# Stores of the scan's matrices and of the inverses issued by GpSimd instead of SyncE, in a hybrid DeltaNet, retention and attention encoder layer

## The chip, the cores and the metric

The kernel runs on one core of one Trainium2 chip. The core has TensorE (PE; its weight loads are listed as PEld), VectorE (DVE), ScalarE (ACT), GpSimd (POOL) and SyncE (SP). SP computes nothing; in this kernel it issues nearly all transfers. In the profile, transfers issued by SP are on queue q1 (hardware_dynamic) and those issued by GpSimd on q0 (software_dynamic); both are carried out by the core's 16 DMA engines. Each engine takes its instructions strictly in the order in which the program lists them for that engine, and waits at the head of its queue until the semaphores it needs are up.

The metric is device time in microseconds for one execution. Several runs are taken, and their median counts.

## What is computed

The reference applies one encoder layer to two sequences (1024 and 256 tokens of width 1024), with the same weights. After an RMS norm, one matrix multiplication projects to the inputs of three groups of heads; their outputs are gated, joined, multiplied by `w_out` and added to the input; a gated embedding term and a last RMS norm follow.

```
xn   = rms_norm(h, norm_g);  proj = xn @ w_in
A (6 heads): q, k, v = silu(conv5(a_qkv)); q, k normalized to length 1
             o = deltanet(q, k, v, beta, g) + the same on the reversed sequence
B (6 heads): retention, forward and reversed, then a head norm
C (4 heads): attention in a window of 128 to each side, with sink and ALiBi
h = h + concat(A, B, C, each times silu(gate)) @ w_out
h = h + (p @ w_ple) * sigmoid(h @ w_pg);  y = rms_norm(h, final_g)
```

The part around the change is group A. The gated delta rule works on chunks of 64 tokens:

```
gamma[c,s] = exp(decay[c] - decay[s]) for s <= c
T  = I + strict_lower((k*beta) k^T * gamma)       # 64 x 64 for each chunk and head
u, w = T^-1 (v*beta),  T^-1 (k*beta*exp(decay))
per chunk, in order:  v_new = u - w S
                      o = (q*exp(decay)) S + (q k^T * gamma) v_new
                      S = S * chunk_decay + (k*exp(decay_last - decay))^T v_new
```

So each chunk needs three matrices beside the inverse of T: the decayed queries, the masked products of q and k, and the decayed keys. The kernel calls them l2. They and the inverses go through DRAM: a preparation writes them, and the scan over the chunks reads them back.

## The kernel before

All products with the big weights are done in float32 as three products of a high and a low part. The kernel runs through these stages, with their approximate place in the profile:

- Load and normalize the input, transpose it to `xh` and `xl` (up to about 40 us).
- The products for the queries, keys and values of group A, with convolution, SiLU and normalization (L510 to L566). The order is `[3, 4, 5, 0, 1, 2, 6, 7, 8]` (L509): keys, queries, and last the values, which are transposed and stored to `VTD`. All nine come ahead of the preparation; the last ends about 218.
- The preparation, `prep_stream` (L569 to L627), about 218 to 347, interleaved by `spread` with ten other products of the input (`PP`, L37). It takes the ten blocks of 128 tokens from the last to the first, and each for two directions d. For each of the 20 pairs: GpSimd loads rows of decays into `DJ[d]` (L591; one tile for each direction), PE spreads them over 128 partitions (L595, the product sb), ScalarE makes the exponentials `ge` (L598, L601), VectorE multiplies the Gram products (L580, in the PSUM bank `sa`) with them into `at` (L609) and into `l2` (L611 to L613), and GpSimd copies the last decay (`elc`, L614). Then SP issues nine stores: four of `at` to `AGD` (L616, for the inversion), one to `ADD_` (L618, for the join), and four of `l2` to `L2D` (L620 for the upper 64 partitions, L623 three times for the lower). `at` and `l2` have two buffers each. In the profile `L2D` is l2d, `AGD` agd, `ADD_` ad, `YDD` yd and the tile `l2` is l.
- After five blocks, `invert(g)` (L399 to L426) for a group g of five blocks and both directions: the 32 x 32 diagonal blocks are read back from `AGD` (L402), VectorE inverts 120 of them for each direction (L411 to L421; the first instruction is one multiplication over 120x2048), and two stores write them to `YDD` (L426). A store takes 120 partitions with 32 rows of 32 elements each, out of rows of 33 elements. `invert(1)` runs between the pairs of the second five blocks and ends at 363; `invert(0)` follows and ends at 447.
- The scan, `scan_stream` (L751), from about 350 to 770: four `join`s (L652) for group 1, each making a part of the full 64 x 64 inverses from `YDD` (yn, L662, transposed to xn at L666) and `ADD_` (an, L659), then 20 steps for both directions (L695 to L749), in which SP loads l2, the inverse and the values, and GpSimd scales values (L702) and states (L726). `weave` and `fill` put window attention, the remaining products and retention beside it. Attention lets GpSimd cast queries (`qh`, L827).
- `w_out`, gate and last norm (about 790 to the end).

What sets the order: the generators hand over pieces in the order of their planned lengths (`T_PREP` = 10.0 for a block of the preparation, `T_JOIN` = 5.0, `T_STEP` = 10.0 and so on), and the framework's planner, which simulates the program (L47: `TCARGS = dict(schedule_with_timeline_sim=True)`), then lays out one fixed sequence for each engine. A piece marked `tc.high_priority()` (the loads at L402) is put ahead.

Through the helper `mm` nearly all products have line 86 in the profile, and through `tt` nearly all two-input operations have line 89; the tile names tell them apart.

Of the kernel before, what the change touches and what calls it, by code (L numbers as in the profile page):

```python
# [53 lines left out]
def encoder_kernel(ctx: ExitStack, tc: tile.TileContext, I, O, dbg=None, upto=99):  # L54
    nc = tc.nc
    uid = [0]

    def nm(s):
        uid[0] += 1
        return f"{s}_{uid[0]}"  # L60

    def bc(ap, shape):
        return ap.to_broadcast(list(shape))
# [5 lines left out]
    def ps(tag):  # L69
        return psp.tile([128, 512], F32, tag=tag, name=nm(tag))  # L70
# [14 lines left out]
    def mm(out, lhsT, rhs, start=True, stop=True):  # L85
        nc.tensor.matmul(out, lhsT, rhs, start=start, stop=stop)  # L86

    def tt(eng, out, a, b, op):
        eng.tensor_tensor(out=out, in0=a, in1=b, op=op)  # L89
# [30 lines left out]
    ot = big.tile([128, 8, PADW], F32, tag="OT", name="ot")  # L120
# [35 lines left out]
    def acc():  # L156
        wide.append(wide.pop(0))
        return ps(wide[-1])
# [216 lines left out]
    L2D = [[tc.dram_tile([2, 128, 3, 3, 64], F32, name=f"l2d{d}_{b}") for b in range(NB)] for d in range(2)]  # L375
# [3 lines left out]
    YDD = [[tc.dram_tile([120, 32, 32], F32, name=f"yd{d}_{g}") for g in range(2)] for d in range(2)]  # L379
# [5 lines left out]
    T, B = slice(0, 64), slice(64, 128)  # L385
# [11 lines left out]
    IREG = (0, 1)  # L397

    def invert(g):  # L399
        for d in range(2):  # L400
            with tc.high_priority():
                nc.sync.dma_start(out=ot[0:120, IREG[d], 0:1056].rearrange("p (a b) -> p a b", a=32),  # L402
                                  in_=AGD[d][g].rearrange("q c p r x -> (q c p) r x"))

        def two(o0, o1, *dims):

            a = ot[0:120, IREG[0], o0:o0 + 1]
            return bass.AP(a.tensor, a.offset, [list(a.ap[0]), [(IREG[1] - IREG[0]) * PADW + o1 - o0, 2], *([list(e) for e in dims])])

        y, yd = two(0, 0, (33, 32), (1, 32)), two(32, 32, (0, 32), (33, 32))  # L410
        tt(V, y, y, yd, MUL)  # L411
        yield 4.2
        for s in range(1, 31):
            na, nb = s, 31 - s
            t3 = two(1056, 1056, (nb, na), (1, nb))

            c = two(s, 33 * (32 - s) + 31 - s, (33, na), (0, nb))
            r = two(33 * s + s + 1, 33 * (31 - s), (0, na), (1, nb))
            o = two(s + 1, 33 * (32 - s), (33, na), (1, nb))
            tt(V, t3, c, r, MUL)  # L420
            tt(V, o, o, t3, ADD)  # L421
            if s % 3 == 0:
                yield 2.8
        V.memset(two(0, 0, (34, 32)), 1.0)
        for d in range(2):
            nc.sync.dma_start(out=YDD[d][g], in_=ot[0:120, IREG[d], 0:1056].rearrange("p (a b) -> p a b", a=32)[:, :, 0:32])  # L426

    def weave(*run):

# [66 lines left out]
    with tc.tile_pool(name="pa", reuse_waits="tile", bufs=2) as pa:  # L496
# [13 lines left out]
        for i, ti in enumerate(order):  # L510
# [18 lines left out]
            if ti < 6:  # L529
                p, isq = ti % 3, ti < 3  # L530
# [17 lines left out]
                if not isq:  # L548
                    nc.sync.dma_start(out=KND[:, :, p, :].rearrange("c p t -> p c t"),
                                      in_=kq[:, p, 0, :].rearrange("p (c t) -> p c t", c=NC))  # L550
            else:
                p = ti - 6
                for b0 in range(0, NB, 4):
# [7 lines left out]
                    for r in range(2):  # L561
# [4 lines left out]
                                      in_=vt[:, 0:nb].rearrange("p b r e -> p (b r) e"))  # L566
        if dbg:
            dbg("kq", kq)
        def prep_stream():  # L569
            for b in reversed(range(NB)):  # L570
                tb = slice(b * 128, (b + 1) * 128)
                g3 = []
                for r in range(2):
                    tk = slice(b * 128 + 64 * r, b * 128 + 64 * r + 64)
                    gram = ps("sa")
                    g3.append(gram[:, 0:384].rearrange("p (q w) -> p q w", q=3))
                    for p in range(3):
                        for h in range(2):
                            rw, o = slice(64 * h, 64 * h + 64), slice(64 - 64 * h, 128 - 64 * h)
                            mm(g3[r][o, p, :].rearrange("p (w t) -> p w t", w=2), kq[rw, p, 0, tk], kq[rw, p, :, tk])  # L580
                kt = ps("tr")
                kt3 = kt[:, 0:384].rearrange("p (q w) -> p q w", q=3)
                for p in range(3):
                    nc.tensor.transpose(kt3[:, p, :], kq[:, p, 0, tb], ident)
                kc = pa.tile([128, 2, 3, 64], F32, tag="kc", name=nm("kc"), bufs=1)
                for r in range(2):
                    for h, rw in ((1, T), (0, B)):
                        S.copy(kc[rw, r], kt3[64 * r:64 * r + 64, :, 64 * h:64 * h + 64])
                for d in range(2):
                    for l in range(2):  # L590
                        nc.gpsimd.dma_start(out=DJ[d][2 * l:2 * l + 2], in_=DRD[d][6 * b:6 * b + 6, l].rearrange("n (s t) -> s n t", s=2))  # L591
                    ge = pa.tile([128, 2, 2, 3, 64], F32, tag="ge", name=nm("ge"))
                    for i in range(2):
                        pd = ps("sb")
                        mm(pd[:, 0:384], SD[i], DJ[d].rearrange("r n t -> r (n t)"))  # L595
                        if i == 0:
                            for n in range(6):
                                S.activation(out=ge[:, 0, n // 3, n % 3], in_=pd[:, 64 * n:64 * n + 64], func=AF.Exp,  # L598
                                             bias=negd[:, d, 2 * b + n // 3, n % 3:n % 3 + 1])
                        else:  # L600
                            S.activation(out=ge[:, 1].rearrange("p c q t -> p (c q t)"), in_=pd[:, 0:384], func=AF.Exp)  # L601
                    at = pa.tile([128, 2, 3, 2, 33], F32, tag="at", name=nm("at"), bufs=AB)
                    l2 = pa.tile([128, 2, 3, 3, 64], F32, tag="l2", name=nm("l2"))
                    last = 63 if d == 0 else 0
                    gl = ge[:, 0, :, :, last:last + 1]
                    el = ge[:, 1, :, :, last:last + 1]
                    S.copy(at[:, :, :, :, 32], bc(nbeta[:, d, 2 * b:2 * b + 2, :].unsqueeze(3), [128, 2, 3, 2]))
                    for r in range(2):
                        tt(V, at[:, r, :, :, 0:32], g3[r][:, :, 0:64].rearrange("p q (w t) -> p q w t", w=2),  # L609
                           ge[:, 0, r].rearrange("p q (w t) -> p q w t", w=2), MUL)  # L610
                        tt(V, l2[:, r, 1], g3[r][:, :, 64:128], ge[:, 0, r], MUL)  # L611
                    tt(V, l2[:, :, 2], kc, bc(gl, [128, 2, 3, 64]), MUL)
                    tt(V, l2[:, :, 0], kq[:, :, 1, tb].rearrange("p q (c t) -> p c q t", c=2), ge[:, 1], MUL)  # L613
                    G.tensor_copy(elc[:, d, 2 * b:2 * b + 2, :], el.rearrange("p c q t -> p c (q t)"))  # L614
                    for q in range(4):
                        nc.sync.dma_start(out=AGD[d][b // 5][q, 2 * b % 10:2 * b % 10 + 2].rearrange("c p r x -> r (c p) x"),  # L616
                                          in_=at[32 * q:32 * q + 32, :, :, q % 2, :].rearrange("r c p x -> r (c p) x"))
                    nc.sync.dma_start(out=ADD_[d][b // 5][2 * b % 10:2 * b % 10 + 2].rearrange("c p q w t -> p c q w t"), in_=at)  # L618

                    nc.sync.dma_start(out=L2D[d][b][:, T].rearrange("r p a q t -> p r (a q t)"),  # L620
                                      in_=l2[T].rearrange("p r a q t -> p r (a q t)"))
                    for a, a2 in ((0, 1), (1, 0), (2, 2)):
                        nc.sync.dma_start(out=L2D[d][b][:, B, a2].rearrange("r p q t -> p r (q t)"),  # L623
                                          in_=l2[B, :, a].rearrange("p r q t -> p r (q t)"))
                    yield T_PREP / 2
                if b % 5 == 0:
                    yield from invert(b // 5)  # L627


        for _ in spread((10 * T_PREP + 2 * 32.2, prep_stream()), length(PP)):  # L630
            pass
# [504 lines left out]
    with tc.tile_pool(name="fw", reuse_waits="tile", bufs=2) as fw:  # L1136
# [21 lines left out]
        for gi in range(2):  # L1158
            c0 = WSEQ[gi][1]
            w = wf.pop()  # L1160
            for i, b in enumerate(range(NB) if gi else FO):
                tk = slice(b * 128, (b + 1) * 128)
                p = acc()
# [22 lines left out]
        for gi in range(2):  # L1186
# [10 lines left out]
            for b in range(NB):  # L1197
                tk = slice(b * 128, (b + 1) * 128)
                end = gi == 1 and b == NB - 1
                for j, (o, n) in enumerate(((0, 256), (256, 256)) if end else ((0, 512),)):  # L1200
                    cs = slice(o, o + n)
                    p = acc()
# [50 lines left out]
```

## Time and profile before

| | us |
|---|---|
| Median of three runs (1092.92 to 1097.69) | 1095.28 |
| The profiled execution | 1089.95 |
| Its span, first to last instruction | 1088.2 |
| Issuing of l2d stores by SP, first to last | 221.4 to 346.8 |
| Issuing of yd stores by SP, two pairs | 362.7 and 447.1 |
| Mean granted TensorE clock | 0.963 |

How to read it: busy shares are means over the whole span, while the change touches only the preparation and the start of the scan. For these, the table of stages and the instructions in order of time are the views to look at. In a line of the latter stand the start, the length, the engine (SPq is SP's queue), the source line, the operation, what it writes and reads, the count and, in brackets, how long the engine stood idle before it and what ended that. The granted clock is the share of full speed that TensorE was allowed. Instructions that issue transfers are not counted as busy time of an engine, and a transfer's time to landing is given where it is known.

### The profile page before, as it was taken

What the parts mean: (1) busy time and instruction counts of PE and PEld (TensorE: products, weight loads), DVE (VectorE), ACT (ScalarE), POOL (GpSimd) and SP (SyncE); (2) the same over time, 40 slices, a digit from 0 to 9 for tenths busy, and PEclk for the clock granted to TensorE, in tenths of its full rate; (3) what the DMA queues carried; (4) which work ended last, traced back from release to release, by engine and by line L of the source; (5) the groups of instructions that cost most, each with busy time, mean ns of one, the idle gap of its engine ahead of it and who ended that gap; (6) DMA issues with size and microseconds to landing.
All of it is one profiled execution on the core that took longest, in us unless ns stands there. A gap on an engine that the chain in (4) does not pass through costs nothing.

```text
span 1088.2 us, 20996 instructions
## 1 busy us (share of the span) xinstructions
PE 1016.4 (93%) x7859; PEld 810.3 (74%) x7859; DVE 626.0 (58%) x1303; ACT 513.6 (47%) x1194; POOL 241.5 (22%) x406
## 2 busy tenths in 40 slices
PE   4999999999798789999998899989799999999996
PEld 4768878888687677877786777767567888888885
DVE  6766676454688588755566764665873333412333
ACT  8476776577467444443444322323341121534544
POOL 2001000022122111221233325554441000112311
PEclk9999999999899889999999799999879999999998
DMA  8112112377778734553555434555461430300211
GB/s 257 38 44 69 45 39 59 74 176 162 184 169 215 162 83 111 118 140 89 121 140 135 117 85 139 147 141 153 126 212 49 171 100 1 97 1 11 98 78 77
DMA packets 199071, 120.57 MB, mean 111 GB/s; under 512 B 105906, under 2 KB 180442, under 8 KB 198970
## 3 DMA queue, kind: packets, MB, share of 16 engines
q1 hardware_dynamic: 194074, 118.97, 41.1%
q8 instruction: 62, 1.02, 0.4%
q0 software_dynamic: 4896, 0.27, 0.4%
q14 instruction: 39, 0.32, 0.1%
HBM read 76.26 MB, written 42.91 MB: 110 GB/s over the span
## 4 chain that ended last, share of the span: by engine, by line
PE 45%; DVE 4%; DMA 2%; POOL 1%; issue 1%; ACT 1%; SPq 0%; DVEq 0%; POOLq 0%; ACTq 0%
PE mm L86 19%; PE sa L86 14%; PE sb L86 6%; PE tr L86 3%; DVE ot L968 2%; PE tr L850 1%; PE tr L1175 1%; POOL oo L89 1%; DMA oo<-od 1%; PE tr L949 1%; DMA od<-os 0%; DMA ot<-in_x_prompt 0%; DMA oo<-ond 0%; PE sa L1034 0%; DVE sab L1020 0%
## 5 line engine op out<-in xcount | busy, mean ns | idle before, releaser
L86 PE MATMUL mm<-xh,whi 128*128 128x512 f32 x720 | 265.6, 369 | 3.5 <-ACT ot L520 1.1
L86 PE MATMUL mm<-xl,whi 128*128 128x512 f32 x720 | 263.2, 366 | 0.0
L86 PE MATMUL mm<-xh,wlo 128*128 128x512 f32 x720 | 261.2, 363 | 0.0
L86 PEld LDWEIGHTS mm<-xh,whi 128*128 128x128 f32 x720 | 137.3, 191 | 29.1 <-ACT ot L520 2.2
L86 PEld LDWEIGHTS mm<-xl,whi 128*128 128x128 f32 x720 | 137.4, 191 | 20.7 <-issue 0.7
L86 PEld LDWEIGHTS mm<-xh,wlo 128*128 128x128 f32 x720 | 137.2, 191 | 20.7 <-issue 0.5
L89 DVE TENSOR_TENSOR ot<-ot 128x1284 f32<-128x1284 f32 (+16 forms) x131 | 85.7, 654 | 23.1 <-ACT ot L102 15.1
L89 DVE TENSOR_TENSOR wlo<-raw,whi 128x1024 fp32r<-128x1024 f32 (+1 forms) x56 | 57.4, 1028 | 32.1 <-ACT whi L149 19.8
L86 PE MATMUL mm<-whi,xh 128*128 128x512 f32 (+1 forms) x168 | 67.9, 406 | 0.6 <-ACT xh L1040 0.4
L86 PE MATMUL mm<-whi,xl 128*128 128x512 f32 (+1 forms) x168 | 67.4, 401 | 0.3 <-DVE xl L89 0.3
L86 PE MATMUL mm<-wlo,xh 128*128 128x512 f32 (+1 forms) x168 | 67.3, 401 | 0.0
L86 PE MATMUL sa<-wlo,xh 128*128 128x512 f32 (+1 forms) x160 | 62.8, 392 | 0.0
L86 PE MATMUL sa<-whi,xl 128*128 128x512 f32 (+1 forms) x160 | 62.6, 391 | 0.0
L86 PE MATMUL sa<-whi,xh 128*128 128x512 f32 (+1 forms) x160 | 62.4, 390 | 0.0
L525 DVE SCALAR_TENSOR_TENSOR ot<-ot,cols 128x1284 f32<-128x1284 f32 x36 | 55.9, 1554 | 0.6
L89 DVE TENSOR_TENSOR sgm<-sb,sgm 128x512 f32<-128x512 f32 (+1 forms) x21 | 14.0, 666 | 72.6 <-ACT sgm L102 60.2
L86 PE MATMUL sa<-sv,l 128*64 128x64 f32 (+1 forms) x912 | 47.0, 238 | 7.4 <-DVE sv L732 5.4
L86 PEld LDWEIGHTS sa<-sv,l 128*64 128x64 f32 (+1 forms) x912 | 36.7, 144 | 18.7 <-DVE sv L732 7.2
L89 POOL TENSOR_TENSOR sv<-sv,elc 64x192 f32<-64x192 f32 x72 | 38.9, 540 | 49.4 <-PE sa L86 26.7
L89 POOL TENSOR_TENSOR ot<-ot,sgm 128x512 f32<-128x512 f32 x19 | 25.5, 1342 | 100.0 <-DVE sgm L89 98.6
L89 POOL TENSOR_TENSOR vt<-vt,sab 128x192 f32<-128x192 f32 x40 | 23.2, 587 | 84.7 <-DMA vt<-vtd 67.7
L86 PEld LDWEIGHTS mm<-whi,xh 128*128 128x128 f32 x168 | 32.4, 194 | 8.2 <-ACT xh L1040 0.6
(302 smaller groups left out, 1975.5 us busy)
## 6 DMA issues: line engine op xcount, KB each, us to landing
raw<-in_w_in SPq DMA_DIRECT2D x28, 512.0 KB, 3.8
l<-l2d SPq DMA_DIRECT2D x40, 288.0 KB, 3.0
l2d<-l SPq DMA_DIRECT2D x20, 288.0 KB
l2d<-l SPq DMA_DIRECT2D x60, 96.0 KB, 3.0
xt<-in_x_prompt SPq DMA_DIRECT2D x8, 512.0 KB, 6.8
ot<-in_x_prompt SPq DMA_DIRECT2D x8, 512.0 KB
raw<-in_w_pg SPq DMA_DIRECT2D x16, 256.0 KB, 3.1
yp<-ot SPq DMA_DIRECT2D x8, 512.0 KB, 2.6
```

Of the source, the lines that this page charges most:

```text
L86: nc.tensor.matmul(out, lhsT, rhs, start=start, stop=stop)
L89: eng.tensor_tensor(out=out, in0=a, in1=b, op=op)
L525: V.scalar_tensor_tensor(out=Y[:, 0:1284], in0=R[:, j:j + 1284], scalar=cw(ti, j), in1=Y[:, 0:1284], op0=MUL, op1=ADD)
L850: nc.tensor.transpose(pt[:, k * 128:(k + 1) * 128], pr[:, k * 128:(k + 1) * 128], ident)
L949: nc.tensor.transpose(pt[:, 0:128], bk[:, b * 128:(b + 1) * 128], ident)
L968: V.scalar_tensor_tensor(out=st[r, b2, h], in0=st[r, b, h], scalar=gs[r, 2 * p + h:2 * p + h + 1], in1=kvt[r, b, h], op0=MUL, op1=ADD)
L1175: nc.tensor.transpose(pt[:, k * 128:(k + 1) * 128], hb[:, b, (n * 4 + k) * 128:(n * 4 + k + 1) * 128], ident)
```

## The change

Three calls that issue stores move from `nc.sync` to `nc.gpsimd`; sizes, layouts and order in the source stay. Four instructions for each of the 20 pairs (80 in all, 11.5 MB) and four for the inverses (1.9 MB) are concerned. The stores to `AGD` and `ADD_` stay with SP, and so do all the loads that read `L2D` and `YDD`.

```
         V.memset(two(0, 0, (34, 32)), 1.0)
         for d in range(2):
-            nc.sync.dma_start(out=YDD[d][g], in_=ot[0:120, IREG[d], 0:1056].rearrange("p (a b) -> p a b", a=32)[:, :, 0:32])
+            nc.gpsimd.dma_start(out=YDD[d][g], in_=ot[0:120, IREG[d], 0:1056].rearrange("p (a b) -> p a b", a=32)[:, :, 0:32])
...
-                    nc.sync.dma_start(out=L2D[d][b][:, T].rearrange("r p a q t -> p r (a q t)"),
+                    nc.gpsimd.dma_start(out=L2D[d][b][:, T].rearrange("r p a q t -> p r (a q t)"),
                                       in_=l2[T].rearrange("p r a q t -> p r (a q t)"))
                     for a, a2 in ((0, 1), (1, 0), (2, 2)):
-                        nc.sync.dma_start(out=L2D[d][b][:, B, a2].rearrange("r p q t -> p r (q t)"),
+                        nc.gpsimd.dma_start(out=L2D[d][b][:, B, a2].rearrange("r p q t -> p r (q t)"),
                                           in_=l2[B, :, a].rearrange("p r q t -> p r (q t)"))
```

## The prediction

> **What bounds the kernel now.** I read the page first, for the span and for the share of each engine.
>
> ```profile
> span 1088.2 us, 20996 instructions
> PE 1016.4 (93%) x7859; PEld 810.3 (74%) x7859; DVE 626.0 (58%) x1303; ACT 513.6 (47%) x1194; POOL 241.5 (22%) x406
> ```
>
> TensorE (PE) is busy 93% of the span, so only time in which PE stands still, or runs at a lower clock, can be won. The table of stages says where. Its columns: stretch and length, busy time and count of PE, PEld, DVE, ACT and POOL, the granted TensorE clock, the busy share of the DMA engines, GB/s.
>
> ```profile
> 219.00:292.00 73.00, 66.61 (x431) 55.70 (x431) 35.71 (x79) 48.97 (x149) 16.36 (x33) 0.99 0.79 180
> 292.00:354.00 62.00, 57.14 (x350) 47.52 (x348) 53.80 (x122) 39.43 (x115) 14.24 (x31) 0.94 0.80 187
> 354.00:386.00 32.00, 23.19 (x127) 17.78 (x128) 20.15 (x44) 13.00 (x29) 9.50 (x9) 0.77 0.71 152
> 386.00:560.00 174.00, 171.65 (x2151) 136.20 (x2148) 119.35 (x298) 77.37 (x181) 36.09 (x54) 0.99 0.47 112
> ```
>
> The moved stores are issued between 221 and 368, and two more at 447. In these stages PE stands still for 6.39 us (219 to 292), 4.86, 8.81 and 2.35. The waits of PE between 219 and 460 name four stalls that make up most of that:
>
> ```profile
> PE tr L850 <- DVE pr L847: 5.3, 2, 5.1
> PE sa L86 <- DVE l L89: 5.2, 1, 5.2
> PE sb L86 <- DVE bias L790: 4.3, 1, 4.3
> PE sb L86 <- DVE xn L666: 2.3, 1, 2.3
> ```
>
> Around them stand granted clocks of 0.77 and 0.94. The change can pay only through these stalls and the low clock behind them. The first question is therefore which of them hangs on the queue that loses work.
>
> **What leaves SP.** The instructions on the two tensors (minimum/median/maximum ns in the queue):
>
> ```profile
> L623 SPq DMA_DIRECT2D l2d<-l x60: 574/613/1674, 222.2 to 346.8; - x60
> L620 SPq DMA_DIRECT2D l2d<-l x20: 580/581/709, 221.4 to 344.7; - x20
> L426 SPq DMA_DIRECT2D yd<-ot x4: 884/2549/4231, 362.7 to 448.1; - x4
> ```
>
> By the medians 60 x 0.613 + 20 x 0.581 = 48.4 us of SP's queue go in the 125 us of the preparation, and the four yd stores, 10.2 us at the median of 2.549, in two bursts. SP is hardly ever empty there, but PE is, so nearly all of these 48 us are worth nothing. They count where a late SP is what PE finally waits for.
>
> **The stall at 286.6 (5.16 us).** In order of time, SP, then VectorE, then PE:
>
> ```profile
> 274.64 1.24 SPq L623 DMA_DIRECT2D l2d<-l  x2
> 275.92 3.41 SPq L616 DMA_DIRECT2D agd<-at  x4
> 282.77 0.34 SPq L402 DMA_DIRECT2D ot<-agd  x1
> ```
> ```profile
> 269.45 1.78 SPq L616 DMA_DIRECT2D agd<-at  x4
> 274.32 0.21 ACT L607 COPY at<-nbeta 128x12 f32<-128x12 f32 x1 [0.55 <-DVE at L89]
> 287.37 3.82 DVE L89 TENSOR_TENSOR ot<-ot 120x2048 f32<-120x2048 f32 x1 [3.77 <-DMA ot<-agd]
> 291.77 2.83 PE L86 MATMUL sa<-kq 64*64 64x128 f32 x24 [5.16 <-DVE l L89]
> ```
>
> The first inversion's input (agd) is stored from `at`, read back at L402, and VectorE waits 3.77 us for it at the head of its queue. The l2 products behind it, which free the sa bank for PE's next gram product, come late by as much. `at` is whole at 274.53, but SP is at its l2d stores until 275.88; the four agd stores then take 3.41 us, where the four before took 1.78. Without the l2d stores in SP's ring they would go from 274.6 to 276.4 instead of ending at 279.33: 2.9 us earlier. The load, VectorE and PE follow one for one, and the stall falls to 5.16 - 2.9 = 2.3 us. VectorE's own idle time (3.77) caps the gain at 3.8, and 0 is the floor if the stores, now side by side in two rings, drain no sooner; I take 2.9, since both delays stand in SP's own rows.
>
> The clock comes on top:
>
> ```profile
> 276.00:286.00 10.00, 9.11 (x51) 7.35 (x48) 2.51 (x7) 6.09 (x22) 1.60 (x5) 1.00 0.78 199
> 292.00:297.00 5.00, 5.00 (x31) 4.29 (x30) 4.72 (x16) 3.46 (x13) 1.29 (x3) 0.51 0.61 132
> 353.00:358.50 5.50, 5.27 (x13) 4.01 (x14) 5.22 (x10) 3.72 (x6) 2.43 (x5) 0.51 0.73 217
> 281.72 0.82 PE L86 MATMUL sb<-dj,sd 128*128 128x384 f32 x2 [0.89 <-ACT ge L598]
> ```
>
> After the stall of 5.16 us the clock is 0.51 for 5 us, so 5.0 x 0.49 = 2.5 us of work is lost; the same after the 4.3 us at 348. After 0.89 us of idling (281.72) it stays 1.00. A remaining 2.3 us lies between. I take the loss as gone; if it stays, the gain is 2.9 alone. The Trainium skill, "TensorE: Matmul & The Clock Gate", Part 1, lets the clock fall after an idle window of about 3.4 us; by it 2.3 us mostly escapes, though the window runs free. The three rows agree with that rule. Sum of this stall: 2.9 + 2.5 = 5.4 us, between 0 and 6.3.
>
> **The stalls at 370 and 385, which the inverses' stores sit in.**
>
> ```profile
> 362.75 5.28 SPq L426 DMA_DIRECT2D yd<-ot  x2
> 368.13 3.96 SPq L472 DMA_DIRECT2D gd<-sg  x1
> 372.19 2.67 SPq L402 DMA_DIRECT2D ot<-agd  x2
> 374.92 1.96 SPq L662 DMA_DIRECT2D yn<-yd  x4
> ```
> ```profile
> 447.14 5.03 SPq L426 DMA_DIRECT2D yd<-ot  x2
> ```
> ```profile
> 384.57 0.68 DVE L666 STREAM_TRANSPOSE xn<-yn 128x480 f32<-128x480 f32 x1
> ```
>
> The first two stores (362.75) hold SP for 5.28 us and the gate's store behind them for 3.96; ACT, VectorE and then PE (5.1 us) wait for that gate store. With them gone from SP's ring, most of the 3.96 us and so most of this stall goes. But PE then meets the join's product sooner, which needs xn, and xn (384.57) needs yd stored, agd loaded and yn read back. These move only if the stores land sooner. So PE's 8.8 us of waiting up to 386 are moved to the wait for xn, not won: 0 us, up to about +5 if the planner finds other matmuls for the place, below 0 by what the stores are slower on GpSimd.
>
> **What GpSimd pays.** No row shows such a store on its queue. The nearest:
>
> ```profile
> L591 POOL DMA_DIRECT2D dj<-drd x40: 548/548/598, 98.8 to 324.2; - x40
> L371 POOL DMA_DIRECT2D drd<-dr x2: 535/542/549, 96.3 to 103.3; - x2
> L262 POOL DMA_DIRECT2D sd<-onesbd x8: 487/487/725, 3.2 to 7.3; - x8
> q0 software_dynamic: 896, 0.03, 2.2%
> dj<-drd POOLq DMA_DIRECT2D x8, 3.0 KB, 3.8
> ```
> ```profile
> l2d<-l SPq DMA_DIRECT2D x60, 96.0 KB, 3.0
> ```
>
> Eight dj loads made the 896 packets of q0 in this stretch (262 to 292): 112 each, 96 if 16 of them are the completion signals, which would be 32 bytes a packet. The one-row sd load costs 487 ns, the 96-packet dj load 548: 61 ns for about 95 packets, 0.65 ns each. An l2d store has 128 rows (64 partitions by 2): 0.57 us. A yd store has 120 x 32 = 3840 rows of 128 bytes: 0.49 + 3840 x 0.65 ns = 3.0 us. If the whole 548 ns were packets, 5.7 ns each, it would be 0.73 and 21.9 us; if rows cost nothing, 0.49. I take 0.57 and 3.0, because three forms of very different size differ by only 61 ns. Then 80 x 0.57 = 46 us are added to a POOL that is busy 16.4 of 73 us and 14.2 of 62: still idle more than a third of the time. Two yd stores take 6.0 us, beside 5.28 on SP; with the 3.0 us of landing that the page gives for an l2d store they are in place at 362.7 + 6.0 + 3.0 = 371.7, before the 374.92 at which yn is read now.
>
> Behind the l2d stores in POOL's order wait the dj loads of the next pairs:
>
> ```profile
> 270.86 1.09 POOL L591 DMA_DIRECT2D dj<-drd  x2 [1.19 <-PE sb L86]
> ```
>
> The pair loaded at 270.86 is used at 281.72 (row above), 10.9 us later, of which 1.1 are issue and 3.8 landing (the 3.8 in the dj row): 6.0 us of slack. Four l2d stores in front cost 4 x 0.57 = 2.3, plus their wait for VectorE's l2. That is covered by the slack; without the cover, PE's sb product would come late by whatever exceeds 6.0. At 447 the second pair of yd stores stands ahead of POOL's casts of qh and its products of the state; PE idles only 2.35 us from 386 to 560, so I cost it at 0 (up to 6.0 if a state product waits for both), and the SP time freed there is worth 0 to 2.
>
> **Sum.** 5.4 + 0 + 0 = 5.4 us, against the profiled execution (1088.2 us of span, 1089.95 in all): 1084.5. The three runs have a median of 1095.28, 5.3 above that execution; the same 5.4 from it gives 1089.9.
>
> **The rivals.**
> *Nothing gained: 1095, within 3.* The DMA engines, not SP, set when agd lands: they are busy 0.79 and 0.80 of these stages (table above), the bytes stay, and an l2d store issued from POOL at the very moment of the agd stores shares the engines with them as before. Then the stall stays at 5.16. Against it: the 1.3 us between 274.53 and 275.92 are SP's own. The Trainium skill, "DMA: Bandwidth & Descriptors", "Issuing engines are not separate DMA queues", speaks for this rival: "Initiating DMAs on multiple engines concurrently will only save the time on the sequencer it takes to initiate the DMA". By that rule alone the stall gives 1.3 us and 1094. Chance 0.26.
> *Slower by the inverses' stores.* If rows cost POOL 2 ns or more each, a yd store takes 8.2 us; both end at 362.7 + 16.4 = 379.1, and 3.0 us later yn can be read, at 382.1 instead of 374.92. PE in its fixed order then stands at the join 7 us longer, which eats the 5.4. At 4 ns (15.9 us each) it is 362.7 + 31.8 + 3.0 = 397.5, 22.6 us late, less 5.4: 17 slower, 1112. It decides from about 1.8 ns on (5.4 us of lateness). For it: 3840 rows lie far outside the 1 to 96 that the rows cover. Against: their small slope. Chance 0.14.
> *Slower by the order of work.* All queues are laid out by a planner that simulates the program; with the stores on POOL it redraws the order. One more stall like the one at 348 costs 4.3 us plus 5.5 x 0.49 = 2.7 of clock: 7.0, and without the gain at 286 the time is 1102. It decides where a dj load lies behind l2d stores by more than its 6.0 us of slack. Chance 0.14.
> That the change doesn't do what it says I leave out: both tensors are plain float32 copies and the edited lines name the queue.
>
> **How the numbers follow.** The forecast has 0.46, around 1090, from 1092.4 (clock loss stays) down to 1080, where the stalls at 370 and 348 or the wait at 385 shrink too (5 us more each at most). 0.5% is 5.5 us, about what a measurement of this kernel can tell from no change, and the sum lies right at it. What I left at nothing can mostly add, so of the 0.46 I give 0.37 to faster by more than that and 0.09 to no change; of the first rival 0.22 to no change, 0.03 to faster and 0.01 to slower; of the slower ones 0.26 to slower and 0.02 to no change. Faster 0.40, same 0.33, slower 0.27. The range 1080 to 1106 leaves out the far part of the yd rival and a little at each end.
>
> **What would show it.** Right: the first agd stores of the group's last pair follow `at` at once and take about 1.8 us; VectorE's wait for ot<-agd is under 1.5 us; PE's longest wait near 290 is under 3 us and the clock there stays 1.00; POOL's l2d stores last 0.5 to 0.8 us and its yd stores 2 to 5; the wait for xn grows as the one for pr goes. Wrong: yd stores above 8 us with yn late; dj loads that land after PE needs them; agd landing no sooner; or a new stall in 219 to 460 on an instruction that had none.

## The result, and the profile after

The median of 12 executions after is 1106.6 us; the kernel before, timed in turn with it on the same chip, has 1093.0 (12 executions). The ratio is **1.0113, 95% interval 1.0083 to 1.0144**: the change costs about 12 us, where 5.4 were expected to be won. The profiled execution after takes 1107.3 us, of which 1105.6 are the span, against 1090.0 and 1088.2.

The page of the kernel after, its span and the shares of the engines:

```profile
span 1105.6 us, 21050 instructions
PE 1023.7 (93%) x7859; PEld 816.3 (74%) x7859; DVE 622.1 (56%) x1303; ACT 512.4 (46%) x1194; POOL 291.8 (26%) x490
```

TensorE does the same 7859 matmuls. POOL has 84 instructions more, which are the moved stores: on GpSimd, unlike on SP, the page counts instructions that issue transfers as busy time. It is busy 50 us longer; the prediction had reckoned 46 for the matrices' stores and 12 for the inverses'. The same table of stages as before:

```profile
219.00:292.00 73.00, 68.71 (x437) 57.40 (x436) 29.41 (x69) 49.48 (x150) 38.16 (x70) 0.99 0.76 176
292.00:354.00 62.00, 54.95 (x334) 44.72 (x332) 50.59 (x108) 28.92 (x93) 30.28 (x53) 0.96 0.64 153
354.00:386.00 32.00, 23.37 (x101) 18.93 (x102) 18.52 (x49) 17.97 (x41) 15.90 (x27) 0.89 0.82 179
386.00:560.00 174.00, 162.62 (x1902) 128.61 (x1900) 118.70 (x294) 75.62 (x177) 39.10 (x52) 0.95 0.45 107
```

PE's busy time up to 386 is the same in sum (147.0 us in the first three stretches, 146.9 before). From 386 to 560 it is 162.6 where it was 171.7, and 249 fewer matmuls are done. The loss becomes visible only behind the stores. What PE waits for between 219 and 460:

```profile
PE mm L86 <- ACT sz L468: 19.9, 7, 10.3
PE sb L86 <- ACT ge L598: 7.4, 4, 2.1
PE sa L86 <- DVE l L89: 2.2, 2, 2.0
```

Of the four stalls that the prediction listed only the one for l is left among these, with 2.2 us instead of 5.2. A wait that was 0.8 us before, for ScalarE's copy of a gate (sz), is now 19.9, and 10.3 of it is one stall. In order of time, VectorE, ScalarE, PE:

```profile
391.06 3.83 DVE L89 TENSOR_TENSOR ot<-ot 120x2048 f32<-120x2048 f32 x1 [2.10 <-DMA ot<-agd]
397.31 0.69 DVE L89 TENSOR_TENSOR sg<-sg,sz 128x512 f32<-128x512 f32 x1
398.04 0.37 ACT L468 COPY sz<-mm 128x256 f32<-128x256 f32 x1 [2.45 <-DVE sg L89]
398.46 0.80 PE L86 MATMUL mm<-xh,whi 128*128 128x512 f32 x1 [10.27 <-ACT sz L468]
```

The second inversion's first operation waits for its agd at the head of VectorE's queue, and the gate's product, on which ScalarE and then PE wait, stands behind it. The inversion itself is late because the whole preparation is. The last agd store and the last load of the scan's matrices, in the kernel after:

```profile
L616 SPq DMA_DIRECT2D agd<-at x80: 302/439/1234, 218.6 to 362.0; - x80
L697 SPq DMA_DIRECT2D l<-l2d x40: 319/332/1932, 378.3 to 783.5; - x40
```

and in the kernel before:

```profile
L616 SPq DMA_DIRECT2D agd<-at x80: 311/442/1571, 218.6 to 343.2; - x80
L697 SPq DMA_DIRECT2D l<-l2d x40: 319/353/1168, 352.1 to 763.0; - x40
```

The preparation ends 18.8 us later and the scan 20.5 us later. The moved stores themselves, on GpSimd's queue, are no dearer than reckoned:

```profile
L623 POOL DMA_DIRECT2D l2d<-l x60: 592/610/654, 219.1 to 365.2; - x60
L426 POOL DMA_DIRECT2D yd<-ot x4: 1707/1766/1835, 365.7 to 461.1; - x4
```

What is dearer is the time from issue to landing. Stretches 219 to 365 (first two rows) and 355 to 400 of the kernel after; name, queue, count, KB each, median us to landing. Before, agd stood at 2.5 in the first stretch:

```profile
l2d<-l POOLq DMA_DIRECT2D x59, 96.0 KB, 4.0
agd<-at SPq DMA_DIRECT2D x79, 24.8 KB, 4.2
```
```profile
yd<-ot POOLq DMA_DIRECT2D x2, 480.0 KB, 10.8
```

So three causes were possible: the inverses' stores **land** late (10.8 us), the matrices' stores **crowd** SP's small ones (agd 4.2 instead of 2.5), or the **order** that the planner drew anew is worse. The order differs a great deal: with the queue of 84 instructions changed, 1018 of the 5865 matrix instructions that the program gives PE have another place in its sequence (counted from the lists of the two orders that h1 and h4 below carry).

### The profile page after: what moved, and what is told of

Its sections match the earlier page's. It is cut to its first block, busy times and chain, and to the rows that moved or that the text cites. A ratio compares the mean times of both kernels' runs of the same rounds, so it can differ in the third digit from the quotient of the medians.

```text
span 1105.6 us, 21050 instructions
## 1 busy us (share of the span) xinstructions
PE 1023.7 (93%) x7859; PEld 816.3 (74%) x7859; DVE 622.1 (56%) x1303; ACT 512.4 (46%) x1194; POOL 291.8 (26%) x490
## 5 line engine op out<-in xcount | busy, mean ns | idle before, releaser
L86 PE MATMUL mm<-xh,whi 128*128 128x512 f32 x720 | 267.6, 372 | 22.0 <-ACT sz L468 19.9
L86 PE MATMUL mm<-xl,whi 128*128 128x512 f32 x720 | 266.0, 369 | 0.0
L86 PE MATMUL mm<-xh,wlo 128*128 128x512 f32 x720 | 264.4, 367 | 0.0
L86 PEld LDWEIGHTS mm<-xh,whi 128*128 128x128 f32 x720 | 139.6, 194 | 48.2 <-ACT sz L468 22.0
L86 PEld LDWEIGHTS mm<-xl,whi 128*128 128x128 f32 x720 | 139.8, 194 | 20.9 <-issue 0.7
L89 DVE TENSOR_TENSOR ot<-ot 128x1284 f32<-128x1284 f32 (+16 forms) x131 | 83.0, 634 | 25.0 <-ACT ot L102 15.1
L623 POOL DMA_DIRECT2D l2d<-l x60 | 36.3, 606 | 18.3 <-DVE l L89 18.0
```

What stands on the lines that cost most here:

```text
L623: nc.gpsimd.dma_start(out=L2D[d][b][:, B, a2].rearrange("r p q t -> p r (q t)"), in_=l2[B, :, a].rearrange("p r q t -> p r (q t)"))
```

## The experiments

All ratios are to the kernel before, timed in turn on the same chip. The chips differ: the kernel before had a median of 1092.2 beside h1 to h4, 1092.5 beside h5 to h8, 1088.9 beside e1, e2, e4 and h10, and 1092.5 beside n1, n5 and e6 (the table gives the value beside the kernel after). So the ratios are what to compare from one group to another. "Last agd" and "last l" are the last starts of lines 616 and 697 in each profile, as in the rows above.

| kernel | stores on GpSimd | order | us | ratio (95%) | last agd | last l |
|---|---|---|---|---|---|---|
| before | none | its own | 1093.0 | 1 | 343.2 | 763.0 |
| after | both | drawn anew | 1106.6 | 1.0113 (1.0083 to 1.0144) | 362.0 | 783.5 |
| h1 | both | of before, held | 1092.8 | 0.9989 (0.9964 to 1.0014) | 341.3 | 769.5 |
| h2 | inverses | of before, held | 1093.5 | 1.0001 (0.9972 to 1.0029) | 346.6 | 772.5 |
| h3 | matrices | of before, held | 1087.7 | 0.9955 (0.9933 to 0.9977) | 344.0 | 765.2 |
| h4 | none | of after, held | 1111.4 | 1.0177 (1.0133 to 1.0220) | 373.3 | 788.1 |
| h5 | both | of after, one exchange | 1100.4 | 1.0058 (1.0027 to 1.0090) | 360.7 | 779.1 |
| h6 | both | of before up to the scan | 1097.4 | 1.0041 (1.0017 to 1.0065) | 340.5 | 776.9 |
| h7 | both | of before from the scan on | 1105.2 | 1.0096 (1.0071 to 1.0121) | 363.9 | 782.3 |
| h8 | matrices; inverses on ScalarE | of before, held | 1087.0 | 0.9940 (0.9919 to 0.9962) | 340.6 | 763.3 |
| e1 | matrices | drawn anew | 1103.9 | 1.0140 (1.0107 to 1.0174) | 360.3 | 782.1 |
| e2 | inverses | drawn anew | 1090.0 | 1.0011 (0.9991 to 1.0030) | 344.8 | 772.2 |
| e4 | none | drawn anew | 1096.1 | 1.0068 (1.0042 to 1.0094) | 344.9 | 771.5 |
| h10 | both | of after, two exchanges | 1101.8 | 1.0131 (1.0095 to 1.0166) | 359.0 | 771.9 |
| n1 | both, dj on SP | drawn anew | 1095.2 | 1.0036 (1.0013 to 1.0058) | 345.5 | 770.4 |
| n5 | matrices, dj on SP, inverses on ScalarE | drawn anew | 1097.8 | 1.0045 (1.0026 to 1.0064) | 345.0 | 768.9 |
| e6 | 60 of the 80 matrices' stores | drawn anew | 1098.6 | 1.0063 (1.0039 to 1.0087) | 343.8 | 774.1 |

### The order held: queue and order taken apart

A list of the order in which the planner had laid out the kernel before (per engine, as positions in the program) is put behind the program, and each instruction gets an edge to the one ahead of it on its engine. Such an edge orders the two; it is no wait. Instructions whose engine was changed are passed over, and the planner finds their place. All others come out in the listed order: in h1 and h3 PE, VectorE and ScalarE have the sequence of before, in h4 that of after.

```python
def hold_order(tc):
    ...
    for e in ("PE", "DVE", "Activation", "Pool", "SP"):
        n, k, prev = v[at], 0, None
        for d in v[at + 1:at + 1 + n]:
            k += d
            i = ins[k]
            if str(i.engine) != "EngineType." + e:
                continue
            if prev is not None:
                tc.add_manual_dep(i, prev.name, mybir.DependencyInfo(
                    mybir.DependencyClass.NoSync, mybir.DependencyReason.DATA), reason="order of before")
            prev = i
        at += 1 + n
```

**h1**, both stores moved, order of before:

> Both sets of stores on GpSimd, as in the kernel after, but each engine's other instructions are held in the order of the kernel before (a list of that order, as edges that only order instructions of one engine). Landing theory (the inverses' stores land 10 to 13 us after their issue, where SP's two were over in 11.6 together): yn is read some 10 us later, xn is as late, PE stands some 10 us longer near 385, the time is 1101 to 1106. Crowding theory (the matrices' stores delay SP's agd and gate stores by 1.7 us each): VectorE and ScalarE wait more from 219 to 365 whatever the order, 1097 to 1106. Order theory (the planner's redrawn order is the loss): with the old order the loss is gone, 1088 to 1095.

**h2**, only line 426 on `nc.gpsimd`, order of before:

> Only the four stores of the inverses on GpSimd, all else in the order of before. Landing theory: the preparation ends as before (last l2 store near 347), yn is read at 382 to 386 instead of 375, and PE stands 7 to 10 us longer near 385: 1100 to 1104. Crowding theory and order theory: 1091 to 1096, no change.

**h3**, only lines 620 and 623 on `nc.gpsimd`, order of before:

> Only the 80 stores of the matrices on GpSimd, all else in the order of before. Crowding theory: agd lands in about 4.2 us (2.5 before), VectorE's wait for it at 287 does not shrink, PE idles 3 us or more longer from 219 to 354: 1096 to 1103. Landing theory and order theory: no loss, 1093, or the 3 to 5 us of gain that the prediction saw at the stall of 286: 1088 to 1093.

**h4**, the list is that of the kernel after, all stores on `nc.sync`:

> All stores back on SP, but each engine's other instructions held in the order of the kernel after. Order theory: the order alone brings the loss, 1102 to 1108, with a stall of PE near 398 behind the first inversion's wait for agd. Landing and crowding theories: 1090 to 1097, at most a few us from an order that was not made for it.

The order theory holds in all four, though h4 is 3.4 us above its range and h3 0.3 below. With the order of before the same move costs nothing that can be told (0.9989); with the order of after and no store moved the whole loss is there (1.0177, against 1.0113 with the stores moved). Whether the move even pays in that order is open, since the two intervals just overlap. h4's waits of PE from 219 to 460 name the same wait as in the kernel after, larger:

```profile
PE mm L86 <- ACT sz L468: 28.0, 6, 14.9
```

The crowding is real, but the time shows no cost of it. In h3, agd lands as late as in the kernel after, and this kernel is the faster one. Stretch 219 to 365 of h3:

```profile
agd<-at SPq DMA_DIRECT2D x80, 24.8 KB, 4.2
```

The late landing is real too, and small. PE's wait for xn in h1, then in h3, where the inverses' stores are on SP:

```profile
PE sb L86 <- DVE xn L666: 7.0, 1, 7.0
```
```profile
PE sb L86 <- DVE xn L666: 1.9, 1, 1.9
```

The way to it can be read from SP's queue: the loads of the next inversion (L402) overwrite `ot` and so wait for the yd stores. SP stands 9.9 us at them in h1 and 1.9 before, and the reading of yn comes right behind. PE waits 5.1 us more in h1 than in h3, and h1's median is 5.0 us above h3's on the same chip, though the two intervals overlap. By itself (h2, ratio 1.0001) the loss can't be told from nothing, though its wait for xn is 6.8. So a price of the late landing isn't shown. Where h3's 0.45% comes from isn't settled either: PE idles as much as before (72.4 us of the span, 71.8 before). The mean granted clock is higher in its profiled execution (0.969 against 0.963), but over all executions it is 0.964 against 0.963, a difference within their spread.

### Which part of the order: two halves, one exchange, another queue

**h5**, the kernel after with one exchange in its list: on VectorE `sg` ahead of the inversion's first operation.

> The kernel after, stores on GpSimd, with one exchange in its order: on VectorE the gate's product (sg, at 397.3 in its profile) stands ahead of the second inversion's first operation (391.1), which waits for agd. ScalarE has that gate ready at 391.6. If head-of-line waiting behind the inversion is what the order costs, PE's wait of 10.3 us at 398 falls to 4 or 5 and the time by 4 to 8, to 1099 to 1103. If instead the late preparation and scan (18 to 20 us later than before) are what costs, the wait moves to the join or the scan and the time stays at 1104 to 1109.

**h6** and **h7**, both stores moved; the edges only among the instructions written ahead of the scan, or only among those from there on:

```python
[[k for k in q if k < 3209] for q in order]
[[k for k in q if k >= 3209] for q in order]
```

> Both sets of stores on GpSimd. The order of before is held only for the instructions written ahead of the scan (the preparation, the inversions, the products beside them); the rest is drawn by the planner. If the loss is in the order of the preparation: 1090 to 1097. If it is in the order of the scan and of the products beside it: 1102 to 1110.

> Both sets of stores on GpSimd. The order of before is held only for the join, the scan and what is written behind them; the preparation is drawn by the planner. If the loss is in the order of the preparation: 1100 to 1110. If it is in the order of the scan and of the products beside it: 1090 to 1097.

**h8**, as h3, and line 426 on `nc.scalar`:

> The order of before held for all else; the matrices' stores on GpSimd, the inverses' stores on ScalarE. If the gain of the kernel with only the matrices moved (1087.7) is SP's freed queue, and the inverses' stores lost it again on GpSimd by their late landing (PE's wait for xn 7.0 against 1.9), then on ScalarE, which idles more than half of that stretch, they land as early as on SP and the gate's store behind them on SP goes 4 us sooner: wait for xn under 4, wait for pr under 3, 1083 to 1088. If ScalarE stands 5 us at the two stores and the gates behind it come late: 1088 to 1095.

h6 against h7: holding the preparation takes away two thirds of the loss (1.0041), holding the scan hardly any (1.0096, the interval overlaps that of the kernel after). h6 is slightly above its expected range and its interval lies above 1, so some of the loss is in the rest of the order.

h5 came out at 1100.4, inside its range, but not by its mechanism: the wait was to fall to 4 or 5 us and is 9.5. ScalarE and PE in h5:

```profile
395.44 0.51 ACT L839 ACTIVATE pr<-pr,mx 128x256 f32<-128x256 f32 x1 [4.05 <-DVE mx L838]
395.95 0.35 ACT L468 COPY sz<-mm 128x256 f32<-128x256 f32 x1
396.35 0.80 PE L86 MATMUL mm<-xh,whi 128*128 128x512 f32 x1 [9.47 <-ACT sz L468]
```

The gate's product now comes at 390.9, but ScalarE's copy stands behind an exponent that waits for a maximum (mx), and that maximum stands behind the same inversion. **h10** moves the maximum ahead as well:

> The order of after with two exchanges: on VectorE the gate's product (sg) and the maximum (mx) for which ScalarE stood at 395.4 both stand ahead of the second inversion's first operation. Then nothing that the copy sz on ScalarE waits for is behind that operation any more: PE's wait near 397 falls from 9.5 to about 6, the rest being the gate's store that ScalarE waits for. If that wait costs what it lasts, the time is 3 to 4 below the kernel with one exchange, 1095 to 1098; if the late scan sets the end, it stays at 1100.

PE's wait there falls to 2.9 us, more than expected, yet the time doesn't follow:

```profile
388.99 0.79 PE L86 MATMUL mm<-xh,whi 128*128 128x512 f32 x1 [2.91 <-ACT sz L468]
```

Its median is 1101.8, ratio 1.0131, no better than the kernel after by the ratio (its profiled execution, 1097.3 us, is the shortest of its six). So the stall of 10.3 us, the largest in the profile, is mostly a place where the lateness shows: in h5 it stayed and the ratio fell, in h10 most of it went and the ratio didn't fall. The intervals of h5 and h10 don't overlap, and why h5 is the faster one stays open; the two were timed on different chips.

h8 has the lowest ratio here, 0.9940, not to be told from h3's. Its inverses' stores go out on ScalarE, and yn is read at 374.4, as in the kernel before, instead of 378.9 in h1.

```profile
374.38 2.70 SPq L662 DMA_DIRECT2D yn<-yd  x4
```
```profile
378.93 1.96 SPq L662 DMA_DIRECT2D yn<-yd  x4
```

The first row is of h8, the second of h1. Of the rest of its expectation, the wait for xn is under 4 us as expected (3.5). The wait for pr is gone from its list of waits; three of 1.4 us and less for pts and one of 3.2 for sz have come in its place.

### The planner left free

**e1**: lines 620 and 623 on `nc.gpsimd`. **e2**: only line 426. **e4**: the kernel before with one number changed:

```diff
-T_PREP = 10.0
+T_PREP = 9.6
```

> The kernel after with the inverses' stores back on SP; the planner draws the whole order anew. With before's order held, the same move gave 1087.7. Order theory: what it costs depends only on the order drawn. If the matrices' stores alone make the planner draw the late preparation (last agd store near 360 instead of 341), 1100 to 1110; if it keeps the early one, 1086 to 1094. Landing theory: 1086 to 1093 in either case.

> Only the inverses' stores on GpSimd; the planner draws the whole order anew. With before's order held, the same move gave 1093.5. Order theory: 1092 to 1097 if the preparation stays early (last agd store near 341), 1100 to 1110 if it comes late. Landing theory: 1100 to 1106.

> No store is moved; one number by which the program weaves the preparation between the products (T_PREP) is 9.6 instead of 10.0, which changes about as much of TensorE's order as the change did. Order theory: a redraw alone can move the time by as much as the change did, in this case by anything from 0 to 17 us up, with the time following the end of the preparation. Landing and crowding theories: 1090 to 1096.

The matrices' stores alone bring the whole loss (e1), the inverses' none (e2, against 1100 to 1106 by the landing theory). Same stores, same queue, e1 and h3: 1.0140 and 0.9955. All of that 1.9% is order. And a redraw with no store moved costs 0.7% (e4), though its preparation ends early (344.9): the time doesn't only follow the end of the preparation, as that expectation had it. The expectations of these three were written for a kernel before of about 1093 us, and on this chip it has 1088.9; e2's 1090.0 is below its range for that reason.

### Why the preparation is drawn late

The rival on the order of work had named a deciding point: the dj loads of the next pairs, which queue behind the matrices' stores on GpSimd. The waits of POOL from 219 to 365, before and then after:

```profile
POOL dj L591 <- PE sb L86: 43.1, 16, 5.5
```
```profile
POOL l2d L623 <- DVE l L89: 18.0, 15, 7.7
POOL dj L591 <- PE sb L86: 12.1, 6, 4.7
```

Before, POOL stood at the dj load and issued it as soon as PE had let go of the buffer. After, it stands 15 times at a matrix store until VectorE has made l, and the next dj load can't go ahead of that. These rows alone don't show a loss: h3, which has none, has much the same ones (15.2 us in 10 waits, 12.3 in 8). What they can change is the planner's order. **n1** takes the loads out of that queue:

```diff
-nc.gpsimd.dma_start(out=DJ[d][2 * l:2 * l + 2], in_=DRD[d][6 * b:6 * b + 6, l].rearrange("n (s t) -> s n t", s=2))
+nc.sync.dma_start(out=DJ[d][2 * l:2 * l + 2].bitcast(F32), in_=DRD[d][6 * b:6 * b + 6, l].rearrange("n (s t) -> s n t", s=2).bitcast(F32))
```

> The kernel after with one line more: the loads dj of the preparation's pairs go to SP, so that no load stands behind the matrices' stores on GpSimd; the planner draws the whole order anew. If it is these loads (the deciding point of the rival on the order of work) for which the planner draws the preparation late, its last agd store comes at 340 to 347 instead of 362 and the time is 1088 to 1097 with both sets of stores on GpSimd. If the late preparation has another reason, it stays near 360 and the time at 1102 to 1110.

**n5** has that line and the inverses' stores on `nc.scalar`; **e6** has only line 623 on `nc.gpsimd`, and dj there too:

> As the kernel with dj on SP, and the inverses' stores on ScalarE, so that no other transfer is late behind GpSimd's ring; the planner draws the whole order anew. If both causes found are the whole of it (order of the preparation, late landing of the inverses on GpSimd): 1084 to 1092, as with before's order held (1087.0). If redrawing costs by itself whatever the preparation does: 1094 to 1100.

> Only the 60 stores of line 623 go to GpSimd (those of line 620 and the inverses' stay on SP); dj stays on GpSimd; the planner draws the whole order anew. By the theory of the dj loads it depends on how late the planner draws the preparation: last agd store at 341 to 349 gives 1088 to 1096, one near 360 gives 1100 to 1106.

n1 answers it for the most part. With the loads on SP the planner draws the preparation early again, and with both sets of stores on GpSimd the time is 1.0036:

```profile
L616 SPq DMA_DIRECT2D agd<-at x80: 302/439/3289, 218.5 to 345.5; - x80
```

So taking the dj loads out from behind the matrices' stores takes away two thirds of the loss (1.0113 less 1.0036). Where the last third lies isn't shown. It isn't the moved stores by themselves (h1), but the dj loads on SP were not timed in the order of before. n5 (1.0045) was expected at 1084 to 1092 and missed it; e6 (1.0063) has the early preparation and came out above its range too. n1, n5, e6, h6 and e4, all partly or wholly drawn anew with the preparation early, lie at 1.0036 to 1.0068. Only e2 among such kernels is level with before. What in those orders costs the 0.4 to 0.7% was not looked for further.

## Why the prediction was wrong, point by point

**The step that failed is one that stands nowhere as a number:** the sum was made on the trace of before, as if all engines kept their order. The forecast moves 84 rows from one queue to another and lets the rest follow. h1 is that kernel, and it shows no change (0.9989), so the forecast would have missed its gain there too, by the next point; but the loss is in the order alone (h4, 1.0177). The kernel after is another program from about 243 us on, where ScalarE's operations of L601 and L607 first stand the other way round. The prediction had this as its third rival, with the right mechanism and the right deciding point (dj loads behind the matrices' stores), but gave it 0.14 and priced it as one more stall of 7.0 us. It is no single stall: the preparation ends 18.8 us later and the scan follows, and the ratio is that of 12 us.

**The stall at 286 (5.4 us of gain).** Failed as well, also with the order held. SP in h3, to be read beside the rows of before:

```profile
276.67 2.60 SPq L616 DMA_DIRECT2D agd<-at  x4
279.31 0.45 SPq L618 DMA_DIRECT2D ad<-at  x1
286.16 0.34 SPq L402 DMA_DIRECT2D ot<-agd  x1
```
```profile
276.90 0.21 ACT L607 COPY at<-nbeta 128x12 f32<-128x12 f32 x1 [0.78 <-DVE at L89]
295.48 2.83 PE L86 MATMUL sa<-kq 64*64 64x128 f32 x24 [6.27 <-DVE l L89]
```

The matrices' stores are out of SP's way, and still the agd stores end at 279.3, as before (279.3). `at` is whole only at 277.1 (274.5 before; why wasn't looked for), and the four stores take 2.60 us, where the prediction reckoned 1.78 without the l2d stores in SP's ring. Then it takes 6.9 us until the load can go, where it took 3.4; PE's stall is 6.3 instead of the 2.3 forecast. The prediction took 0 as the floor "if the stores, now side by side in two rings, drain no sooner". They drain later: the floor was below zero. The first rival had it right that SP's queue doesn't set when agd lands. The rule of the Trainium skill that is quoted there ("DMA: Bandwidth & Descriptors", "Issuing engines are not separate DMA queues"), by which only the sequencer's time is saved, agrees with the trace in that nothing lands sooner. The small stores even land 1.7 us later by the median (4.2 against 2.5).

**The clock behind that stall (2.5 us)** went with it: in h3 it is 0.50 from 295.5 to 300.5, as it was 0.51 before from 292 to 297.

**The stalls at 370 and 385 (0).** With the order held, nothing is won, as forecast, but not in the way that was forecast: most of the wait for pr was to go, and it only shrinks from 5.1 to 4.3 in h1, while the wait for xn grows from 2.3 to 7.0.

**GpSimd's price.** A matrix store costs 0.59 to 0.61 us (0.57 forecast), an inverse's 1.77 (3.0 forecast; its 3840 rows cost 0.33 ns each above the 0.49 of a one-row load). The second rival, which wanted more than 2 ns a row, is refuted in its cause. But its consequence, yn late, is half there for another reason: the prediction let a yd store land 3.0 us after its issue, like an l2d store of 128 rows, and it takes 10.8. From the first store's issue to the reading of yn it is 12.2 us in the kernel before (362.75 to 374.92), 15.1 in h1 (363.86 to 378.93) and 11.4 in h8 (363.0 to 374.4). That term was put at 0. PE's wait for xn is 5.1 us longer by it (h1 against h3), and whether the time is, isn't shown (h2).

**The dj loads' slack of 6.0 us.** The row was right and the question wrong: with the order held, the loads behind the stores cost nothing that can be told (h1); what counted was the order that the planner draws when they stand there (n1). What the planner itself reckoned for them was not read. PE's waits ahead of the products sb rose from 1.2 to 7.4 us, but the profile puts them down to ScalarE's exponentials (ge) and not to a dj load; the longest such wait in h1 (3.2 us at 285.1) stands behind ScalarE's wait of 5.1 us for the gate's store.

**The range** (1080 to 1106) ended 0.6 us short of the result: on its slower side it held one stall more, and not a preparation that ends 19 us late.

## What to carry to other kernels

Where a planner lays out the queues, moving one instruction to another engine is two changes: the move, and a new order. Hold the old order and make the move, then hold the new order without it; two runs tell which of them the time belongs to. Here the whole move was worth nothing that can be told (h1) and that of the matrices alone 0.45% (h3), while the new order cost 1.2 to 1.9% (after against h1, e1 against h3). Before giving an engine more stores, look at what stands behind them in its queue (here the loads that start the next step), and treat the longest stall of the slower profile as a symptom until its removal has been timed.

## What the runs showed of the hardware

In this kernel the same stores make fewer packets on GpSimd's queue than on SP's. Stretch 219 to 365, packets, MB and share of the engines' time, in the kernel before and then in h3, which has the same order:

```profile
q1 hardware_dynamic: 46057, 26.29, 75.7%
q0 software_dynamic: 3808, 0.12, 1.9%
```
```profile
q1 hardware_dynamic: 32856, 13.66, 41.0%
q0 software_dynamic: 8288, 11.92, 34.1%
```

GpSimd's queue gained 4480 packets and 11.80 MB, 2.6 KB each, which are the 80 stores. SP's lost 13201 packets and 12.63 MB, about 1 KB each (a little of it is other work at the ends of the stretch). The engines' busy share hardly changed (77.6% and 75.1%), and SP's small agd stores beside them landed in 4.2 us instead of 2.5.

Why they land later isn't shown. That larger packets of the other queue make them wait would fit these rows, and no run tested it alone. e6 bears on it: there only the 60 stores of 96 KB go through GpSimd, in packets of 2.0 KB (2880 more packets, 5.90 MB), and agd lands in 2.6 us. So the delay seems to hang on the 20 stores of 288 KB, whose packets are larger (3.7 KB), or on the bytes as a whole; e6 has another order besides.
